# Mamba2's decays per head and RWKV's key preparation: work moved from GpSimd to VectorE in a two-layer decoder trunk

## The chip, the cores and the metric

The kernel runs on one core of a Trainium2 chip. A core has TensorE (PE in the rows: matmuls; PEld are its weight loads), VectorE (DVE), ScalarE (ACT), GpSimd (POOL) and SyncE (SP, which here issues the DMAs). Each works through its own queue in order and waits for others by semaphores. The metric is the device time of one execution, in microseconds (us), as the median over several runs.

## The reference

Two layers over x of 1024 positions and 1024 features, in float32. Each normalizes, projects to the inputs of three mixers, runs these, multiplies them by a SiLU gate, concatenates, projects back and adds. The first layer has RWKV-7, an S5 state-space model and attention to a memory of 256 entries; the second has Mamba-2, multi-head latent attention (MLA) and the memory attention. The change touches these parts of RWKV-7 and Mamba-2:

```python
def rwkv7_time_mix(p, mu, w0, w2, a0, a2, k_k, k_a, r_k, ln_w, ln_b):
    ...
    log_w = -jax.nn.softplus(-(w0 + jnp.tanh(w_lat) @ w2)) - 0.5
    decay = jnp.exp(-jnp.exp(log_w))
    iclr = jax.nn.sigmoid(a0 + a_lat @ a2)
    kk = (k * k_k).reshape(b, s, h, n).astype(jnp.float32)
    kk = (kk * lax.rsqrt(jnp.maximum(jnp.sum(kk * kk, -1, keepdims=True), 1e-24))).astype(p.dtype)
    k = k * (1.0 + (iclr - 1.0) * k_a)
    ...
    removal = kk * iclr
    def step(state, inp):
        r_t, w_t, k_t, v_t, kk_t, b_t = inp
        sa = -jnp.einsum('bhij,bhj->bhi', state, kk_t)
        state = (state * w_t[:, :, None, :] + sa[..., None] * b_t[:, :, None, :]
                 + v_t[..., None] * k_t[:, :, None, :])
        return state, jnp.einsum('bhij,bhj->bhi', state, r_t)
    ...

def mamba2_ssd(xbc, dt_raw, z, conv_w, conv_b, dt_bias, a_log, d_skip, norm_w):
    ...
    a_cum = jnp.cumsum(a_dt, axis=-1)
    lmat = jnp.exp(segsum(a_dt))
    cb = jnp.einsum('bclgn,bcsgn->bgcls', cc, bc)
    y_diag = jnp.einsum('bgcls,bgjcls,bcsgjp->bclgjp', cb, lmat, xdt)
    decay_states = jnp.exp(a_cum[..., -1:] - a_cum)
    states = jnp.einsum('bcsgn,bgjcs,bcsgjp->bcgjpn', bc, decay_states, xdt)
    ...
    y_off = jnp.einsum('bclgn,bcgjpn,bgjcl->bclgjp', cc, states, jnp.exp(a_cum))
    y = (y_diag + y_off).reshape(b, s, h, p) + xh * d_skip[:, None]
```

`lmat` holds, for each head and chunk of 128 positions, the exponential of the difference of two running sums of the log decay, for a target and an earlier source position.

## The kernel before

**Matmuls.** Every float32 operand of a large product is split into a high and a low part (L405 on ScalarE, L406 on VectorE), and a product takes three matmuls. The large projections are the dense stream: weights w come in by DMA on SP's queue (L331), are split, and are multiplied (L180). The mixers' own products and transposes (L180, L184) stand between.

**What sets the order.** A planner (class Flow) runs the mixers as generators and fixes TensorE's order: each `yield` says how much planned time must pass on TensorE, or which event or PSUM bank must be there, before the generator goes on, and the dense stream fills what is free. TensorE's instructions keep that order. The order in the other engines' queues is set by a scheduler that knows the dependencies and estimated durations; a queue, once built, runs in order.

**RWKV** (about 70 to 950 us of the span). 16 units: eight pairs of heads, each in two halves of 512 positions. For each unit:

- `rw_prep0` makes keys, decays and the removal vectors. kh (tile tg) is the scaled key; its squares are summed per head on TensorE; L588 multiplies the reciprocal of the sum by kh (d2, tile tb). L600 clears a column of ce, L602 forms running sums of the log decays, L607 centres them (cc), and L611 and L613 take exponentials. L614 and L615 pick the factors at chunk ends (fin). L619, L621 and L623 build kr and bm from these; L621 needs L588's result. L624 (ScalarE) and L625 build the mixed key. `half_products` then has TensorE form products of bm and kr into ga.
- `rw_inv0` inverts small triangular blocks: four DMAs of ga to memory (L699), one back into ai (L702), GpSimd's copy L706 of a start value into ti, then 31 pairs of a product (L711) and a subtraction (L713) on ti, the DMA of ti to memory (L715), and four DMAs back into xt (L718). ti and ai have one buffer each.
- `rw_inv1` transposes parts of xt (L728, VectorE) and continues on TensorE.
- `rw_prep1` makes km (L665), and L666 and L668 further operands.
- `rw_seq` runs over the chunks and keeps the state; its L808 (ScalarE) evicts rh, which TensorE reads next.

So GpSimd does the inverses and, between them, L588, L600, L614, L615, L625 and L665.

**Mamba2** (about 1640 to 2090 us). Two groups of eight heads, eight chunks of 128 positions each: 16 calls of `m2_x` and `m2_y`. `m2_x` loads into lm the running sums of the chunk for eight heads, broadcast over the partitions (L1931, three buffers); eb is the exponential of a part of it (L1936). L1937 (GpSimd) subtracts the source position's running sum, one column per head broadcast along the row; L1938 (VectorE) takes the minimum with 0; L1939 (ScalarE) the exponential; L1941 multiplies by the masked product of C and B, on VectorE in odd chunks and on GpSimd in even ones. Then come xdt (L1946), xdec (L1956), and the new state sta (L1962, L1963). `m2_y` has TensorE form the outputs, and VectorE combines them: m2y (L1981, L1982) and xs (L1987, four per chunk). The stream `x()` calls `m2_x` for one chunk after the other.

Of the kernel before, what the change touches and what calls it, by code (L numbers as in the profile page):

```python
# [10 lines left out]
F32 = mybir.dt.float32  # L11
# [3 lines left out]
A = mybir.AluOpType  # L15
# [4 lines left out]
P = 128  # L20
# [245 lines left out]
class K:  # L266
# [303 lines left out]
    def rw_prep0(self, st, p, lat, l2, k, wk):  # L570


        nc, F = self.nc, self.flow
        b3 = lambda ap: ap.rearrange("p (b t) -> p b t", b=4)
        l2h, l2l = l2
        kh = self.pp.tile([P, HT], F32, name="tg", bufs=1)
        nc.scalar.mul(kh, k, self.col("rw_k_k", p))
        sq = self.pp.tile([P, HT], F32, name="tb", bufs=1)
        nc.scalar.square(sq, kh)
        parts = self.pp_parts(sq)  # L580
        yield [BK, ("g", 1)]
        ps = self.bank("g")
        self.head_sums(ps, parts)
        d2 = self.pp.tile([P, HT], F32, name="tb", bufs=1)
        nc.vector.tensor_scalar(d2, ps, 1e-24, None, A.max)
        F.rel("g", 2.0)
        nc.vector.reciprocal(d2, d2)
        nc.gpsimd.tensor_tensor(d2, d2, kh, A.mult)  # L588
        yield ("g", 2)
        pw, pa = self.bank("g"), self.bank("g")  # L590
        for i, o in enumerate((pw, pa)):
            for j, w in enumerate((l2h, l2l)):
                F.matmul(o, lhsT=w[:, i, :], rhs=lat[:, i], start=(j == 0), stop=(j == 1))
        tw = self.pp.tile([P, HT], F32, name="ta", bufs=1)
        nc.scalar.activation(tw, pw, AF.Tanh, bias=self.hw0[:, p:p + 1], scale=0.5)
        F.rel("g", 2.0)
        F.rel("g", 5.0)
        nc.scalar.activation(tw, tw, AF.Identity, bias=1.0)
        ce = self.pp.tile([P, 4, P + 1], F32, name="ce", bufs=1)
        nc.gpsimd.memset(ce[:, :, 0:1], 0.0)  # L600
        for b in range(4):
            nc.vector.tensor_tensor_scan(ce[:, b, 1:P + 1], self.rst, tw[:, b * P:(b + 1) * P], 0.0,  # L602
                                         A.mult, A.add)
        ic = self.pp.tile([P, HT], F32, name="ta", bufs=1)
        nc.scalar.activation(ic, pa, AF.Tanh, bias=self.hw0[:, 8 + p:9 + p], scale=0.5)
        cc = self.pp.tile([P, 4, P + 1], F32, name="cc", bufs=1)
        nc.vector.tensor_tensor(cc, ce, ce[:, :, 64:65].broadcast_to([P, 4, P + 1]), A.subtract)  # L607
        fin = wk.tile([P, 12], F32, name="fin", bufs=4)
        nc.scalar.activation(fin[:, 0:4], ce[:, :, 64], AF.Exp, scale=-KDEC)
        e = ce  # L610
        nc.scalar.activation(e, cc, AF.Exp, scale=-KDEC)  # L611
        em = cc[:, :, 1:P + 1]
        nc.scalar.activation(em, em, AF.Exp, scale=KDEC)  # L613
        nc.gpsimd.tensor_copy(fin[:, 4:8], e[:, :, P])  # L614
        nc.gpsimd.tensor_tensor(fin[:, 8:11], fin[:, 4:7], fin[:, 1:4], A.mult)  # L615
        nc.scalar.activation(ic, ic, AF.Identity, scale=0.5, bias=self.p5)

        kr = wk.tile([P, 4, 2, P], F32, name="kr", bufs=3)
        nc.vector.tensor_tensor(kr[:, :, 0, :], b3(kh), e[:, :, 0:P], A.mult)  # L619

        nc.vector.tensor_tensor(kh, d2, ic, A.mult)  # L621
        bm = b3(kh)
        nc.vector.tensor_tensor(bm, bm, em, A.mult)  # L623
        nc.scalar.activation(ic, ic, AF.Identity, scale=self.col("rw_k_a", p), bias=self.oka[:, p:p + 1])  # L624
        nc.gpsimd.tensor_tensor(k, ic, k, A.mult)  # L625

        ga = wk.tile([P, 4, 2, P], F32, name="ga", bufs=2)
        yield [HA, ("g", 2)]
        self.half_products(bm, kr, 0, ga)
        st.update(fin=fin, kr=kr, ga=ga, e=e, em=em, bm=bm, k2=k)  # L630
# [28 lines left out]
    def rw_prep1(self, st, p, r, v, wk):  # L659

        nc, F = self.nc, self.flow
        b3 = lambda ap: ap.rearrange("p (b t) -> p b t", b=4)
        kr, e, em, bm, k2 = (st[n] for n in ("kr", "e", "em", "bm", "k2"))
        km = st["km"] = wk.tile([P, 4, P], F32, name="km", bufs=2)
        nc.gpsimd.tensor_tensor(km, b3(k2), em, A.mult)  # L665
        nc.vector.tensor_tensor(kr[:, :, 1, :], b3(r), e[:, :, 1:P + 1], A.mult)  # L666

        nc.vector.scalar_tensor_tensor(k2, r, self.col("rw_r_k", p), k2, A.mult, A.mult)  # L668
        parts = self.pp_parts(k2)
        tok = st["tok"] = wk.tile([P, 3, 4, P], F32, name="tok", bufs=2)  # L670

        for i, src in ((0, b3(v)), (1, bm), (2, km)):
            if i == 2:
                yield [BL, ("g", 1)]
                bp = self.bank("g")
                self.head_sums(bp, parts)
                bon = st["bon"] = wk.tile([P, HT], F32, name="bon", bufs=2)
                nc.vector.tensor_tensor(bon, bp, v, A.mult)
                F.rel("g", 2.0)
            yield ("g", 1)  # L680
            tp = self.bank("g", (P, 4, P))
            for b in range(4):
                F.transpose(tp[:, b, :], src[:, b, :], self.ident)
            nc.scalar.copy(tok[:, i], tp)
            F.rel("g", 2.0)
        gr = st["gr"] = wk.tile([P, 4, 2, P], F32, name="gr", bufs=2)
        yield ("g", 2)
        self.half_products(bm, kr, 1, gr)
# [1150 lines left out]

    def m2_open(self, wk):  # L1840
        nc = self.nc
        self.m2w, self.nxs, self.cv, self.lacc = wk, 6, {}, {}
        self.hconv = wk.tile([P, 60], F32, name="hconv")
        o = COFF["conv0"]
        nc.vector.tensor_scalar(self.hconv, self.cols[:, o:o + 60], 0.5, None, A.mult)
        self.hm2n = wk.tile([P, 8], F32, name="hm2n")
        o = COFF["m2_norm_w"]
        nc.vector.tensor_scalar(self.hm2n, self.cols[:, o:o + 8], 0.5, None, A.mult)
        self.one = wk.tile([P, P], F32, name="one")
        nc.vector.memset(self.one, 1.0)  # L1850
        self.ones = {}
        for n in (2048, 384, 256):
            self.ones[n] = wk.tile([P, P], F32, name="ones%d" % n)
            nc.vector.memset(self.ones[n], 1.0 / n)
        self.mincl = wk.tile([P, P], F32, name="mincl")
        nc.gpsimd.memset(self.mincl, 1.0)
        nc.gpsimd.affine_select(out=self.mincl, in_=self.mincl, compare_op=A.is_ge, fill=0.0,
                                base=0, pattern=[[1, P]], channel_multiplier=-1)
        self.sel = wk.tile([P, P], F32, name="sel")
        nc.gpsimd.memset(self.sel, 0.0)  # L1860

        nc.gpsimd.affine_select(out=self.sel, in_=self.sel, compare_op=A.not_equal, fill=1.0, base=-127,
                                pattern=[[0, P]], channel_multiplier=1)
        self.tk = {n: wk.tile([P, 8, 16], F32, name="tk" + n) for n in ("ac", "dt", "et", "dd")}
# [36 lines left out]
    def m2_bc(self, g):  # L1901
# [5 lines left out]
        for c4 in range(0, 8, 4):  # L1907
# [11 lines left out]
            F.rel("g", 1.5)  # L1919
            F.rel("g", 2.0)  # L1920

    def m2_x(self, g, c, st):

        nc, F, wk, tk = self.nc, self.flow, self.m2w, self.tk
        tt, ptt = nc.vector.tensor_tensor, nc.gpsimd.tensor_tensor
        hs = slice(8 * g, 8 * g + 8)
        bc = lambda ap, n: ap[:, c, hs].unsqueeze(2).broadcast_to([P, 8, n])
        v3 = lambda ap: ap.rearrange("p (h q) -> p h q", h=8)
        s = slice(c * P, (c + 1) * P)
        lm = wk.tile([P, 8, P], F32, name="lm", bufs=3)  # L1930
        nc.sync.dma_start(lm, self.acd[hs, s].unsqueeze(0).broadcast_to([P, 8, P]))  # L1931
        eb = wk.tile([P, 4, P], F32, name="eb", bufs=2)
        l2 = lm.rearrange("p (r two) t -> p r two t", two=2)
        for i in range(2):
            r = slice(64 * i, 64 * i + 64)
            nc.scalar.activation(eb[r], l2[r, :, i], AF.Exp)  # L1936
        ptt(lm, lm, bc(tk["ac"], P), A.subtract)  # L1937
        nc.vector.tensor_scalar(lm, lm, 0.0, None, A.min)  # L1938
        nc.scalar.activation(lm, lm, AF.Exp)  # L1939
        cb = self.cbm[:, c].unsqueeze(1).broadcast_to([P, 8, P])  # L1940
        (tt if c % 2 else ptt)(lm, lm, cb, A.mult)  # L1941
        tp = self.bank("g")
        for i in range(4):
            F.transpose(tp[:, i * P:(i + 1) * P], self.cv[4 * g + i][:, s], self.ident)
# [10 lines left out]
        xd = wk.tile([P, 512], F32, name="xdec", bufs=2)  # L1955
        tt(v3(xd), v3(tp), bc(tk["dd"], 64), A.mult)  # L1956
        F.rel("g", 2.5)
        yield [3.0, ("g", 1)]
        sp = self.bank("g")
        F.matmul(sp, lhsT=self.btok[:, c], rhs=xd, start=True, stop=True)  # L1960
        nx = st["next"] = wk.tile([P, 512], F32, name="sta", bufs=3)
# [97 lines left out]
    def m2_streams(self):  # L2059
# [9 lines left out]
        def x():  # L2069
            for g in range(2):  # L2070
                yield [("conv", 8 + g), ("conv", 10 + g), "m2dt"]
                yield from self.m2_bc(g)
                F.done(("bc", g), 0)
                for c in range(8):
                    n = 8 * g + c
                    yield [("conv", 4 * g + 3), ("g", 1)] + ([("y", n - 2)] if n > 1 else [])
                    yield from self.m2_x(g, c, sts[g])
                    F.done(("x", n), 7.0)
# [402 lines left out]
```

## Time and profile before

| what | value |
|---|---|
| time of three runs | 2715.13, 2717.84 (median), 2728.02 us |
| the profiled execution's own time | 2720.39 us |
| its span, first to last instruction | 2718.5 us |
| mean granted TensorE clock | 0.956 of full |
| busy: PE | 2517.2 us (93%), 15058 instructions |
| busy: PEld | 2032.4 us (75%) |
| busy: DVE | 1747.5 us (64%), 3423 instructions |
| busy: ACT | 1248.3 us (46%) |
| busy: POOL | 670.2 us (25%), 1407 instructions |

A row of the profile names the source line (L588), the engine, the operation, and output <- inputs by the program's names, with the output's shape and type and the input's. "x16" is a count. In square brackets, or after a last bar, stands how long the engine had been idle before and what it waited for. "SPq" is a DMA queue of SP. The granted clock (PEclk) is a share of full speed.

### The profile page before, as it was taken

The numbers are of one execution on the slowest core, as the hardware profiler recorded it, in microseconds if no ns is written. First come the engines' busy times: TensorE is split into PE (matmuls) and PEld (weight loads), VectorE is DVE, ScalarE is ACT, GpSimd is POOL, SyncE is SP. The second block draws the span as 40 slices with busy tenths as digits, with TensorE's granted clock in tenths as the row PEclk, the third lists the DMA queues.
The fourth block names the chain that finished last, engine by engine and source line by source line (L and its number), as shares of the span: only waits on it lengthen the run. The fifth ranks groups of instructions, "written<-read, shape, count | busy, mean of one in ns | idle before, by whom it ended". The sixth has DMA issues, their size and how long they took to land. (4 is left out here: it accounts for less than half of the span.)

```text
span 2718.5 us, 42261 instructions
## 1 busy us (share of the span) xinstructions
PE 2517.2 (93%) x15058; PEld 2032.4 (75%) x15058; DVE 1747.5 (64%) x3423; ACT 1248.3 (46%) x2443; POOL 670.2 (25%) x1407
## 2 busy tenths in 40 slices
PE   7899999998999989988999998988999979998997
PEld 5777777786777877776778776767677768887786
DVE  9756666675665536776556357777733987777532
ACT  7444344443443333554443346435344646655443
POOL 3544543544345300010000111251311030000011
PEclk9989999999999989888999999999999999999999
DMA  4433233233332334464674564242445431114543
GB/s 152 130 93 96 90 96 104 86 90 89 95 104 59 88 119 143 137 211 131 196 235 138 165 189 123 71 124 73 109 149 180 142 112 57 57 50 134 179 136 99
DMA packets 263859, 328.27 MB, mean 121 GB/s; under 512 B 88016, under 2 KB 135248, under 8 KB 263136
## 3 DMA queue, kind: packets, MB, share of 16 engines
q1 hardware_dynamic: 260736, 319.39, 38.1%
q0 software_dynamic: 1280, 4.20, 0.5%
q8 instruction: 119, 1.95, 0.3%
q10 hardware_dynamic: 1632, 1.98, 0.3%
q14 instruction: 92, 0.75, 0.1%
HBM read 232.59 MB, written 92.90 MB: 120 GB/s over the span
## 5 line engine op out<-in xcount | busy, mean ns | idle before, releaser
L406 DVE TENSOR_TENSOR wl<-w,wh 128x512 fp32r<-128x512 f32 (+2 forms) x410 | 279.6, 685 | 294.2 <-ACT wh L405 285.8
L405 ACT CAST wh<-w 128x512 fp32r<-128x512 f32 (+2 forms) x410 | 242.2, 594 | 389.1 <-PE mm L180 251.1
L180 PE MATMUL mm<-xhi,wh 128*128 128x512 f32 x832 | 363.0, 436 | 13.2 <-ACT xhi L474 6.8
L180 PE MATMUL mm<-xlo,wh 128*128 128x512 f32 x832 | 339.3, 408 | 4.8 <-DVE xlo L497 2.4
L180 PE MATMUL mm<-xhi,wl 128*128 128x512 f32 x832 | 337.4, 406 | 0.0
L180 PE MATMUL mm<-x1h,wh 128*128 128x512 f32 (+1 forms) x608 | 252.5, 415 | 24.6 <-ACT craw L1829 14.8
L180 PE MATMUL mm<-x1h,wl 128*128 128x512 f32 (+1 forms) x608 | 241.8, 398 | 0.0
L180 PE MATMUL mm<-x1l,wh 128*128 128x512 f32 (+1 forms) x608 | 241.5, 397 | 0.0
L711 POOL TENSOR_TENSOR titmp<-ai,ti 128x60 f32<-128x60 f32 (+24 forms) x496 | 159.9, 322 | 299.8 <-DMA ai<-d_in 262.5
L180 PEld LDWEIGHTS mm<-xhi,wh 128*128 128x128 f32 x832 | 162.2, 195 | 66.8 <-issue 19.9
L180 PEld LDWEIGHTS mm<-xhi,wl 128*128 128x128 f32 x832 | 162.3, 195 | 39.4
L180 PEld LDWEIGHTS mm<-xlo,wh 128*128 128x128 f32 x832 | 162.9, 196 | 36.6 <-DVE xlo L475 5.5
L713 POOL TENSOR_TENSOR ti<-ti,titmp 128x60 f32<-128x60 f32 (+24 forms) x496 | 163.8, 330 | 38.6
L180 PEld LDWEIGHTS mm<-x1h,wh 128*128 128x128 f32 (+1 forms) x608 | 116.8, 192 | 57.1 <-ACT craw L1829 17.6
L180 PEld LDWEIGHTS mm<-x1l,wh 128*128 128x128 f32 (+1 forms) x608 | 116.7, 192 | 27.5 <-issue 3.9
L180 PEld LDWEIGHTS mm<-x1h,wl 128*128 128x128 f32 (+1 forms) x608 | 116.3, 191 | 26.7 <-DVE wl L406 0.2
L180 PE MATMUL mm<-yb,wh 128*128 128x512 f32 x320 | 103.7, 405 | 5.2 <-ACT yb L405 3.8
L800 ACT ACTIVATE sn<-s0c,fin 64x64 f32<-64x64 f32 x128 | 44.1, 345 | 105.5 <-DVE s0c L828 58.3
L786 DVE TENSOR_TENSOR gb<-g,m 128x256 f32<-128x256 f32 x128 | 49.4, 417 | 58.3 <-PE g L180 58.0
L1680 POOL TENSOR_TENSOR sq<-sq,sqt 128x512 f32<-128x512 f32 x14 | 18.1, 1291 | 246.3 <-DMA w<-in_w_ev_out 161.1
L180 PEld LDWEIGHTS mm<-yb,wh 128*128 128x128 f32 x320 | 61.4, 192 | 21.7 <-ACT yb L405 4.2
L419 DVE SCALAR_TENSOR_TENSOR ev<-ev,mm 128x512 f32<-128x512 f32 x72 | 49.0, 681 | 42.7 <-ACT ev L418 42.3
(598 smaller groups left out, 6329.1 us busy)
## 6 DMA issues: line engine op xcount, KB each, us to landing
w<-in_w_ev_in SPq DMA_DIRECT2D x106, 256.0 KB
w<-in_w_od_in SPq DMA_DIRECT2D x82, 256.0 KB
w<-in_w_ev_out SPq DMA_DIRECT2D x64, 256.0 KB
w<-in_w_od_out SPq DMA_DIRECT2D x64, 256.0 KB
rd<-ev SPq DMA_DIRECT2D x50, 256.0 KB
spl<-yd SPq DMA_DIRECT2D x40, 256.0 KB
zod<-ev SPq DMA_DIRECT2D x36, 256.0 KB
ai<-d_in SPq DMA_DIRECT2D x16, 512.0 KB
```

Source lines behind the costliest of these rows:

```text
L180: return self._pe(self.nc.tensor.matmul(out, lhsT=lhsT, rhs=rhs, start=start, stop=stop, **kw), math.prod(rhs.shape[1:]), rhs.dtype)
L405: self.nc.scalar.copy(hi, src)
L406: self.nc.vector.tensor_tensor(lo, src, hi.bitcast(F32), A.subtract)
L419: nc.vector.scalar_tensor_tensor(g, g, 1.0, ps, A.add, A.mult)
L711: eng.tensor_tensor(tm, ai[:, s:s + 1, s + 1:32].broadcast_to([P, n, w]), ti[:, 0:n, s:s + 1].broadcast_to([P, n, w]), A.mult)
L713: eng.tensor_tensor(ti[:, 0:n, s + 1:32], ti[:, 0:n, s + 1:32], tm, A.subtract)
L786: nc.vector.tensor_tensor(gb[:, h], pgs[h], self.m2, A.mult)
L800: nc.scalar.mul(sg[hs], sc[hs, hs], g[hs])
L1680: nc.gpsimd.tensor_tensor(self.sq1, self.sq1, t, A.add)
```

## The change

In RWKV six instructions go from GpSimd to VectorE: L588, L600, L614, L615, L625 and L665. What they compute is unchanged. In Mamba2 the subtraction and the minimum become eight VectorE instructions per chunk, one per head, with the head's column as a per-partition scalar and both operations in one; the mask product is on VectorE in every chunk. The load of lm is asked for one chunk ahead by a new function. Three planned times change: 5.0 in place of 3.0 before the state product, and new waits of 6.0 at the start of the second group and 8.0 before the first chunk of the first. Lines behind L1921 have numbers 6 or 7 higher in the changed kernel (L1987 becomes L1994).

```diff
@@ rw_prep0
-        nc.gpsimd.tensor_tensor(d2, d2, kh, A.mult)
+        nc.vector.tensor_tensor(d2, d2, kh, A.mult)
...
-        nc.gpsimd.memset(ce[:, :, 0:1], 0.0)
+        nc.vector.memset(ce[:, :, 0:1], 0.0)
...
-        nc.gpsimd.tensor_copy(fin[:, 4:8], e[:, :, P])
-        nc.gpsimd.tensor_tensor(fin[:, 8:11], fin[:, 4:7], fin[:, 1:4], A.mult)
+        nc.vector.tensor_copy(fin[:, 4:8], e[:, :, P])
+        nc.vector.tensor_tensor(fin[:, 8:11], fin[:, 4:7], fin[:, 1:4], A.mult)
...
-        nc.gpsimd.tensor_tensor(k, ic, k, A.mult)
+        nc.vector.tensor_tensor(k, ic, k, A.mult)
@@ rw_prep1
-        nc.gpsimd.tensor_tensor(km, b3(k2), em, A.mult)
+        nc.vector.tensor_tensor(km, b3(k2), em, A.mult)
@@ m2_open
-        self.m2w, self.nxs, self.cv, self.lacc = wk, 6, {}, {}
+        self.m2w, self.nxs, self.cv, self.lacc, self.lms = wk, 6, {}, {}, {}
@@ new function
+    def m2_lm(self, g, c):
+        lm = self.lms[g, c] = self.m2w.tile([P, 8, P], F32, name="lm", bufs=3)
+        src = self.acd[8 * g:8 * g + 8, c * P:(c + 1) * P]
+        self.nc.sync.dma_start(lm, src.unsqueeze(0).broadcast_to([P, 8, P]))
@@ m2_x
-        lm = wk.tile([P, 8, P], F32, name="lm", bufs=3)
-        nc.sync.dma_start(lm, self.acd[hs, s].unsqueeze(0).broadcast_to([P, 8, P]))
+        lm = self.lms.pop((g, c))
+        if (g, c) != (1, 7):
+            self.m2_lm(*divmod(8 * g + c + 1, 8))
...
-        ptt(lm, lm, bc(tk["ac"], P), A.subtract)
-        nc.vector.tensor_scalar(lm, lm, 0.0, None, A.min)
+        for h in range(8):
+            nc.vector.tensor_scalar(lm[:, h], lm[:, h], tk["ac"][:, c, 8 * g + h:8 * g + h + 1], 0.0, A.subtract, A.min)
         nc.scalar.activation(lm, lm, AF.Exp)
         cb = self.cbm[:, c].unsqueeze(1).broadcast_to([P, 8, P])
-        (tt if c % 2 else ptt)(lm, lm, cb, A.mult)
+        tt(lm, lm, cb, A.mult)
...
-        yield [3.0, ("g", 1)]
+        yield [5.0, ("g", 1)]
@@ x()
             for g in range(2):
                 yield [("conv", 8 + g), ("conv", 10 + g), "m2dt"]
+                if g == 0:
+                    self.m2_lm(0, 0)
+                yield 6.0 * g
                 yield from self.m2_bc(g)
                 F.done(("bc", g), 0)
+                yield 8.0 * (1 - g)
```

GpSimd's queue in RWKV, between the end of one unit's inverse and the start of the next, before:

```order
L711 TENSOR_TENSOR titmp<-ai,ti 128x8
L713 TENSOR_TENSOR ti<-ti,titmp 128x8
L706 COPY ti<-t_558 128x256
L588 TENSOR_TENSOR tb<-tb,tg 128x512
L614 COPY fin<-ce 128x4
L615 TENSOR_TENSOR fin<-fin 128x3
L625 TENSOR_TENSOR rk<-ta,rk 128x512
L665 TENSOR_TENSOR km<-rk,cc 128x512
L711 TENSOR_TENSOR titmp<-ai,ti 128x31
L713 TENSOR_TENSOR ti<-ti,titmp 128x31
```

The same place in the changed kernel:

```order
L711 TENSOR_TENSOR titmp<-ai,ti 128x8
L713 TENSOR_TENSOR ti<-ti,titmp 128x8
L706 COPY ti<-t_558 128x256
L711 TENSOR_TENSOR titmp<-ai,ti 128x31
L713 TENSOR_TENSOR ti<-ti,titmp 128x31
```

Nothing is left between the copy that opens an inverse and its first step. VectorE's queue in one RWKV unit, as a piece of the difference:

```order
+L588 TENSOR_TENSOR tb<-tb,tg 128x512
 L607 TENSOR_TENSOR cc<-ce 128x516
 L828 SCALAR_TENSOR_TENSOR s0c_584<-g,fin,sn_7122 64x64 x2
+L614 COPY fin<-ce 128x4
 L619 TENSOR_TENSOR kr<-tg,ce 128x4x128
 L666 TENSOR_TENSOR kr<-rr,ce 128x4x128
+L615 TENSOR_TENSOR fin<-fin 128x3
 L621 TENSOR_TENSOR tg<-tb,ta 128x512
 L563 TENSOR_SCALAR bd<-mm,cols 128x1
 L566 SCALAR_TENSOR_TENSOR ev<-mm,cols,ev 128x511
 L623 TENSOR_TENSOR tg<-tg,cc 128x512
+L625 TENSOR_TENSOR rk<-ta,rk 128x512
```

L588 now stands ahead of L607, on the engine that also runs L621, which reads its result. The other rows keep their order. VectorE's queue around a chunk of Mamba2, before:

```order
L1938 TENSOR_SCALAR lm<-lm 128x1024
L1981 TENSOR_TENSOR m2y<-g,eb 128x512
L1982 TENSOR_TENSOR m2y<-m2y,g 128x512
L1963 TENSOR_TENSOR sta<-sta,g 128x512
L1987 SCALAR_TENSOR_TENSOR xs<-xs,cols,m2y 128x128 x4
L1946 TENSOR_TENSOR xdt<-g,tkdt 128x512
L1956 TENSOR_TENSOR xdec<-g,tkdd 128x512
L406 TENSOR_TENSOR wl<-w,wh 128x512
L419 SCALAR_TENSOR_TENSOR ev<-ev,mm 128x512
L1963 TENSOR_TENSOR sta<-sta,g 128x512
L1938 TENSOR_SCALAR lm<-lm 128x1024
L1941 TENSOR_TENSOR lm<-lm,cbm 128x1024
```

In the changed kernel, where L1945 is the instruction per head, L1948 the mask product, and L1988, L1989 and L1994 are L1981, L1982 and L1987 of before:

```order
L1945 TENSOR_SCALAR lm<-lm,tkac 128x128 x3
L1994 SCALAR_TENSOR_TENSOR xs<-xs,cols,m2y 128x128 x4
L1945 TENSOR_SCALAR lm<-lm,tkac 128x128 x5
L406 TENSOR_TENSOR wl<-w,wh 128x512
L419 SCALAR_TENSOR_TENSOR ev<-ev,mm 128x512
L1988 TENSOR_TENSOR m2y<-g,eb 128x512
L1948 TENSOR_TENSOR lm<-lm,cbm 128x1024
L1989 TENSOR_TENSOR m2y<-m2y,g 128x512
L1945 TENSOR_SCALAR lm<-lm,tkac 128x128 x2
L1970 TENSOR_TENSOR sta<-sta,g 128x512
L1945 TENSOR_SCALAR lm<-lm,tkac 128x128 x6
```

The eight instructions of a chunk stand among those of another chunk's output, and the mask product stands between the two halves of m2y.

## Rows read from the trace of the kernel before

**Rows 1.** Waits of VectorE, 60 to 950 us: total us, times, longest.

```profile
DVE tg L621 <- POOL tb L588: 37.5, 9, 6.6
DVE cc L607 <- POOL ce L600: 25.7, 13, 5.6
```

**Rows 2.** Timeline, 674 to 680 us: start us, duration us, instruction, idle before, releaser.

```profile
675.29 0.40 POOL L706 COPY ti<-t 128x256 f32<-128x256 f32 x1 [4.89 <-DMA d_out<-ti]
675.65 1.26 POOL L588 TENSOR_TENSOR tb<-tb,tg 128x512 f32<-128x512 f32 x1
676.94 0.69 DVE L621 TENSOR_TENSOR tg<-tb,ta 128x512 f32<-128x512 f32 x1 [6.62 <-POOL tb L588]
...
678.70 1.11 PE L180 MATMUL g<-rh,xt 128*128 128x64 f32 x4 [5.97 <-ACT rh L808]
```

**Rows 3.** Five stretches: us, busy PE, PEld, DVE, ACT, POOL, PEclk, DMA, GB/s.

```profile
124.00:157.00 33.00, 23.79 (x169) 18.16 (x168) 12.15 (x22) 10.61 (x21) 12.96 (x31) 0.74 0.33 90
297.00:308.00 11.00, 6.75 (x67) 5.29 (x69) 4.26 (x9) 2.69 (x7) 3.45 (x5) 0.69 0.61 179
455.00:485.00 30.00, 24.75 (x194) 19.27 (x192) 14.68 (x38) 9.11 (x20) 9.36 (x24) 0.66 0.33 94
619.00:683.00 64.00, 53.14 (x404) 42.08 (x403) 39.59 (x85) 23.90 (x51) 31.08 (x75) 0.92 0.35 100
780.00:847.00 67.00, 58.60 (x440) 46.41 (x440) 39.21 (x84) 25.49 (x56) 29.71 (x75) 0.92 0.34 95
```

**Rows 4.** RWKV units, products to L728: three quiet, then nine stalled, with sums.

```profile
517.30:568.40 51.10, 51.10 (x426) 41.25 (x425) 37.12 (x82) 21.25 (x46) 23.97 (x68) 1.00 0.29 89
...
sum 155.90, PE 155.49 PEld 125.62 DVE 108.18 ACT 66.31 POOL 72.82; mean PE 51.83 PEld 41.88 DVE 36.06 ACT 22.10 POOL 24.27
...
626.50:685.10 58.60, 52.39 (x412) 41.79 (x411) 38.71 (x83) 23.30 (x50) 26.45 (x70) 0.93 0.33 96
...
sum 516.00, PE 473.36 PEld 376.80 DVE 316.08 ACT 209.13 POOL 236.79; mean PE 52.60 PEld 41.87 DVE 35.12 ACT 23.24 POOL 26.31
```

**Rows 5.** Timeline of SP's DMA queue: the inverse's way back in two units.

```profile
561.97 2.64 SPq L718 DMA_DIRECT2D xt<-d_out  x4
...
675.19 1.80 SPq L718 DMA_DIRECT2D xt<-d_out  x4
```

**Rows 6.** Tile ti: minimum, median, maximum ns, first and last start.

```profile
L711 POOL TENSOR_TENSOR titmp<-ai,ti x496: 209/291/866, 108.7 to 940.1; 128x60 f32<-128x60 f32 x16, 128x28 f32<-128x28 f32 x12, 128x66 f32<-128x66 f32 x11, 128x48 f32<-128x48 f32 x10
```

**Rows 7.** Groups of VectorE by form: busy us, mean ns, idle before, releaser.

```profile
L621 DVE TENSOR_TENSOR tg<-tb,ta 128x512 f32<-128x512 f32 x16 | 11.0, 689 | 37.5 <-POOL tb L588 37.5
L2232 DVE TENSOR_SCALAR pe<-pe,lsm 128x1024 f32<-128x1024 f32 x8 | 6.1, 767 | 0.2
L2232 DVE TENSOR_SCALAR pe<-pe,lsm 128x256 f32<-128x256 f32 x8 | 2.8, 345 | 0.0
L1938 DVE TENSOR_SCALAR lm<-lm 128x1024 f32<-128x1024 f32 x16 | 16.0, 1000 | 12.3 <-POOL lm L1937 12.3
L1941 DVE TENSOR_TENSOR lm<-lm,cbm 128x1024 f32<-128x1024 f32 x8 | 12.8, 1601 | 2.9 <-ACT lm L1939 2.9
L1987 DVE SCALAR_TENSOR_TENSOR xs<-xs,cols,m2y 128x128 f32<-128x128 f32 x64 | 37.7, 646 | 0.1
```

**Rows 8.** Groups of GpSimd by form, in Mamba2.

```profile
L1937 POOL TENSOR_TENSOR lm<-lm,tkac 128x1024 f32<-128x1024 f32 x16 | 31.4, 1965 | 24.0 <-ACT eb L1936 21.5 <-ACT tkac L1889 2.5
L1941 POOL TENSOR_TENSOR lm<-lm,cbm 128x1024 f32<-128x1024 f32 x8 | 20.6, 2578 | 17.8 <-ACT lm L1939 12.0 <-DVE cbm L1917 5.8
```

**Rows 9.** Line L1987's instructions: minimum, median, maximum ns.

```profile
L1987 DVE SCALAR_TENSOR_TENSOR xs<-xs,cols,m2y x64: 332/340/2466, 1761.2 to 1990.6; 128x128 f32<-128x128 f32 x64
```

**Rows 10.** Two stretches of Mamba2, columns as in the five stretches.

```profile
1740.00:1835.00 95.00, 84.95 (x473) 66.51 (x472) 72.75 (x105) 34.82 (x53) 45.56 (x31) 0.95 0.43 117
1905.00:1985.00 80.00, 70.79 (x421) 55.13 (x420) 58.72 (x84) 33.61 (x48) 30.57 (x19) 0.98 0.42 116
```

**Rows 11.** Waits of ScalarE, 1640 to 2090 us.

```profile
ACT eb L1936 <- DMA lm<-acd: 33.9, 8, 8.4
```

## The prediction

> **What bounds the kernel now.** I read the busy times first, then the chain of waits, the stretches where TensorE idles, the waits by engine, and the timeline around each gap. TensorE runs an order fixed at build time and is busy for 93% of the span, so only its idle time and the time at the lower granted clock can be won; the reader is to see which engine ends its waits.
>
> In the RWKV part the waits lead to GpSimd. VectorE waits 37.5 us in 9 places for the product of L588, the longest 6.6 us, and 25.7 us in 13 places at L607 for the little memset of L600 [rows 1]. One such place, instruction by instruction [rows 2]: GpSimd's queue is in order, and its copy L706, which opens the next inverse, waits 4.89 us for the transfer that carries the last inverse out. L588, ready long before, stands behind that copy and takes 1.26 us. VectorE (L621) has waited 6.62 us for it; ScalarE's L624 needs what VectorE makes, L808 stands behind L624 in ScalarE's queue, and TensorE, which needs L808's rh, stood still for 5.97 us. Five stretches hold nearly all such places [rows 3]. They last 33 + 11 + 30 + 64 + 67 = 205 us and TensorE is busy for 167.0 of them: 38.0 idle. Their granted clock is 0.74, 0.69, 0.66, 0.92 and 0.92, where a stretch without a gap shows 1.00 [rows 4]. A lost tenth of a stretch is a tenth of its time, so this is 8.6 + 3.4 + 10.2 + 5.1 + 5.4 = 32.7 us at the 1.2 GHz level. Together 70.7 us, of which 1.86 us for each us of idleness.
>
> In Mamba2 GpSimd's subtraction L1937 (1965 ns) and its mask product L1941 (2578 ns) [rows 8] slow VectorE, which works beside them: L1987 has a median of 340 ns but reaches 2466 [rows 9], and its mean is 646 [rows 7]. Two stretches hold most of TensorE's losses there [rows 10]: 95 + 80 us with 84.95 + 70.79 busy, so 19.3 idle, and 95 x 0.05 + 80 x 0.02 = 6.4 of clock: 25.7 us.
>
> **RWKV: six instructions to VectorE.** TensorE's order is unchanged there. After the change GpSimd holds nothing but inverses, so nothing waits behind L706 any more: the 70.7 us are the gross gain. What is late next is the inverse itself: products to memory, GpSimd's 62 instructions, result back, transposes at L728. Three units without a large stall show what a unit takes with that chain in it: 51.10 us with TensorE always busy and the clock at 1.00 in one, 155.90 over the three, 51.97 each [rows 4]. Nine stalled units take 516.00, 57.33 each. If they become like the three, 516.0 - 9 x 51.97 = 48.3 us go. That is 22.4 less than 70.7; part of the difference lies in the unit ahead of the nine. So the chain takes back between 0 and 22.4 us; I take 18, near the upper end, because the units' rows measure it.
>
> On VectorE each of the 16 units gets L588, L625 and L665, at the 689 ns that L621 takes with the same shape [rows 7], and three tiny ones. A per-column operation takes 345 ns for 256 elements and 767 for 1024 [rows 7], so 0.55 ns an element and some 204 ns before the first. Per unit 3 x 0.69 + 3 x 0.2 = 2.7 us, in all 43. Bounds on TensorE's path: 0, since VectorE is busy for 37.12 us of the quiet unit's 51.10 and TensorE doesn't wait there [rows 4], to all 43. I take 8, a fifth, nearer to that row: L588 stands at the head of the chain to the next products, the others have slack. A gain from VectorE no longer being slowed beside GpSimd's big products lies within the choice. RWKV: 70.7 - 18 - 8 = 45 us.
>
> A rule of the Trainium skill (SBUF — State Buffer, "Who interferes with whom") speaks against this: a VectorE instruction with two SBUF inputs and a GpSimd one that reads SBUF lock each other out, and the later one waits for the whole of the other. By it the three moved products, 2.1 us a unit, could each hold up an inverse step; over 16 units 33 us on the inverse chain, and the sum would be 2693. The spread of L711, 291 ns in the median and 866 at most [rows 6], agrees that it happens.
>
> **Mamba2: decays per head on VectorE.** Removed from GpSimd: 16 subtractions and 8 mask products. VectorE gets 128 instructions of 128 elements: 204 + 128 x 0.55 = 274 ns each, an estimate from the two rows of L2232, so 35.1 us; 8 mask products at 1601 ns, 12.8 us; it loses 16 minima of 1000 ns [rows 7]. It also has a new wait: in the even chunks too the mask product now stands in VectorE's queue behind ScalarE's exponential, and m2y's second half and L1987's successors behind it. For the same wait VectorE shows 2.9 us in 8 chunks [rows 7], GpSimd 12.0 [rows 8]: I take 5. Relief: L1987's 64 instructions cost 37.7 us where 64 medians are 21.8, so up to 16 us; half, 8, since the other half may come from other neighbours. Net 35 + 13 - 16 + 5 - 8 = 29 us more VectorE, over 16 chunks, where it idles 22.3 + 21.3 us in the two stretches [rows 10].
>
> What TensorE gains from it: at best all 25.7 us; at worst nothing, and the 29 us land on it. I take half of the gain, 13: the gaps that VectorE's slowed instructions cause should go, those that wait for the load of lm stay. ScalarE waits 33.9 us for that load in 8 places [rows 11]. It is now asked for a chunk earlier in the program, but it has the same three buffers, each freed by TensorE, and in SP's queue it stands where it stood, with weight loads behind it: I take nothing. The ends are a gain within the 25.7 us, and a loss of one such wait, 8.4 us [rows 11], if a weight load comes to stand behind a load of lm. The waits of 6 and 8 units at the start of each group only set where TensorE's planner puts the first chunk: in TensorE's order its transposes come after 81 matmuls of the dense stream in both kernels. Between pairs of chunks, 45 dense matmuls now stand where 36 stood, unevenly, so the chunks are spread over a longer time: cover for the 29 us.
>
> **Sum.** 2720.4 (the profiled execution's own time, 1.9 above its span) - 45 - 13 = 2662. The median of the runs, 2717.84, is 2.6 below the profiled one, so 2660.
>
> **Rivals.**
> 1. The inverse is late in every unit. For it: from its products to the first result transfer unit 10 takes 675.19 - 626.50 = 48.7 us, the quiet unit 561.97 - 517.30 = 44.7 [rows 4, 5], so units may come out at 51.97 + 4.0 = 56.0. Then 9 x (57.33 - 55.97) = 12 us go, less 8, and with Mamba2's 13 the time is 2701. Against it: in three units it did not happen. The skill's rule above would end between this and the forecast.
> 2. VectorE becomes the bound, and the kernel slower. Added are 43 us in RWKV and 35 + 13 - 16 + 5 = 37 in Mamba2, 80 in all. If each landed on TensorE with its clock, 80 x 1.86 = 149 us would stand against 70.7 + 25.7 = 96: 53 more, 2771. It decides from 96 / 1.86 = 52 us, two thirds of the added work. Against it: VectorE idles 14 us in a quiet unit [rows 4].
> 3. Mamba2 loses: VectorE is busy for 72.75 of 95 us [rows 10] and its 29 us land on TensorE. 2720.4 - 45 + 29 - 2.6 = 2702.
> 4. All losses go and nothing takes their place: 2720.4 - 96 - 2.6 = 2621.
> 5. The change moves queues but not the waits, if what L808 waits for is ScalarE's own order rather than L588: about 2717. Against it: in the row of L621 all 37.5 us end with L588 [rows 7].
>
> **How the numbers follow.** The forecast 0.62, with its own range 2635 to 2690; the late inverse 0.13 (2690 to 2706, most of it the skill's rule and the chain together); Mamba2 losing 0.06; all losses going 0.08; no change 0.04; VectorE the bound 0.07. The range to hold the time 8 times in 10 is 2618 to 2708: it takes in the 2621 and the two cases near 2702. A measurement of this kernel tells 0.5% from no change, 13.6 us, so faster is below 2704.2. Faster: 0.62 + 0.08 + 0.09 + 0.03 = 0.82. Same: 0.04 of the late inverse, 0.03 of Mamba2 losing, 0.04 without change: 0.11. Slower 0.07.
>
> **What would show it.** The waits of VectorE for GpSimd at L621, L607 and L668 are gone, and the five stretches' granted clock is near 1.00. TensorE's gaps that remain in RWKV end at the transposes of L728, up to 3 us each, and those up to 1.8 without a fall of the clock. L588 and its neighbours take about 0.7 us on VectorE, and L711 keeps its median near 291 ns; at over 330 the lock-out of the two engines is real. In Mamba2 the per-head instructions take near 0.27 us and L1994 (L1987 before) keeps to its median. It would be wrong if VectorE is busy for over 45 us of a unit, or if TensorE waits for VectorE's lm in Mamba2 more than it does now.

## The result and the profile after

The changed kernel takes 2695.24 us (median of 4 runs, 2688.09 to 2699.3), the kernel before 2722.93 (4 runs, 2715.13 to 2743.78). The ratio is 0.9892, with a 95% interval of 0.9851 to 0.9933: 29 us faster (18 to 41). 58 us were forecast. The direction was right. The time lies inside the range of 2618 to 2708, but outside the forecast's own 2635 to 2690 and inside that of the first rival, the late inverse (2690 to 2706). Half of the gain is missing, and it is missing in RWKV.

Busy times of the changed kernel, from its page:

```profile
span 2697.5 us, 42287 instructions
...
PE 2520.6 (93%) x15058; PEld 2036.5 (75%) x15058; DVE 1771.6 (66%) x3639; ACT 1249.7 (46%) x2445; POOL 563.2 (21%) x1287
```

The work did move: GpSimd is busy for 107 us less, VectorE for 24 more. The waits that the change was to end are gone. Before, VectorE waited for GpSimd at L621 and L607 [rows 1], and at L668:

```profile
DVE rk L668 <- POOL km L665: 13.1, 6, 5.1
```

The changed kernel has none of the three, and L588 takes 700 ns on VectorE, as forecast. Groups of VectorE by form in the changed kernel:

```profile
L588 DVE TENSOR_TENSOR tb<-tb,tg 128x512 f32<-128x512 f32 x16 | 11.2, 700 | 0.0
...
L621 DVE TENSOR_TENSOR tg<-tb,ta 128x512 f32<-128x512 f32 x16 | 10.9, 680 | 0.0
...
L1945 DVE TENSOR_SCALAR lm<-lm,tkac 128x128 f32<-128x128 f32 x128 | 32.1, 315 | 6.4 <-ACT eb L1943 6.4
L1948 DVE TENSOR_TENSOR lm<-lm,cbm 128x1024 f32<-128x1024 f32 x16 | 20.3, 1271 | 1.8 <-ACT lm L1946 1.5
L1994 DVE SCALAR_TENSOR_TENSOR xs<-xs,cols,m2y 128x128 f32<-128x128 f32 x64 | 20.2, 374 | 0.0
```

L621's 37.5 us of waiting [rows 7] are 0.0 now. Yet TensorE got little of it. Two windows between the same instructions of TensorE in both kernels, the bulk of RWKV (6000 matmuls) and Mamba2 with what stands beside it (2300); columns as in [rows 3]. The kernel before:

```profile
143.50:948.70 805.20, 763.89 (x6001) 610.55 (x6000) 509.85 (x1101) 326.40 (x699) 374.35 (x1029) 0.96 0.31 91
1649.60:2167.80 518.20, 472.42 (x2302) 380.10 (x2301) 350.71 (x549) 247.86 (x410) 134.00 (x111) 0.96 0.39 120
```

The changed kernel:

```profile
135.40:954.60 819.20, 780.09 (x6002) 624.21 (x6001) 530.32 (x1182) 326.85 (x698) 322.19 (x946) 0.94 0.31 90
1645.50:2145.70 500.20, 468.71 (x2302) 378.07 (x2301) 347.35 (x669) 246.41 (x411) 87.00 (x87) 0.97 0.41 124
```

Mamba2 is 18 us shorter. RWKV starts 8 us earlier and ends 6 later: TensorE idles for 39.1 us there, 41.3 before, at a clock of 0.94 in place of 0.96. Single profiles scatter: the same RWKV code ended at 948.7 us here and at 962.5 in the profile of the kernel with Mamba2's part alone. So what RWKV is worth is taken from timed runs below. What the traces do show is that the wait moved. Waits of TensorE in that stretch (total us, times, longest), the kernel before:

```profile
PE g L180 <- ACT rh L808: 16.7, 4, 6.0
PE g L180 <- DVE xn L728: 12.4, 15, 2.5
PE g L180 <- DVE s0c L828: 9.6, 3, 4.7
```

and the changed kernel:

```profile
PE g L180 <- DVE xn L728: 35.4, 21, 7.2
PE g L180 <- ACT ta L616: 1.2, 1, 1.2
```

The waits for rh and s0c, at the end of the chain from L588, are gone, and the wait for L728, the transposes of the inverse's result, has grown from 12.4 to 35.4 us, with 7.2 for the longest. Here is that wait in unit 1, followed back through the queues (start us, duration us, instruction, idle before). First ScalarE's eviction of ga, from the timeline of the changed kernel:

```profile
130.95 1.07 ACT L654 COPY ga<-g 128x512 f32<-128x512 f32 x2
```

SP's queue:

```profile
135.43 0.57 SPq L715 DMA_DIRECT2D d_out<-ti  x1
...
140.16 1.80 SPq L718 DMA_DIRECT2D xt<-d_out  x4
...
144.50 2.08 SPq L699 DMA_DIRECT2D d_in<-ga  x4
...
149.33 0.54 SPq L702 DMA_DIRECT2D ai<-d_in  x1
...
186.04 0.56 SPq L715 DMA_DIRECT2D d_out<-ti  x1
...
190.77 1.81 SPq L718 DMA_DIRECT2D xt<-d_out  x4
```

GpSimd's inverse, then VectorE and TensorE behind it:

```profile
160.32 0.24 POOL L711 TENSOR_TENSOR titmp<-ai,ti 128x31 f32<-128x31 f32 x1 [19.66 <-DMA ai<-d_in]
```

```profile
192.50 1.40 DVE L728 STREAM_TRANSPOSE xn<-xt 32x256 f32<-32x256 f32 x3 [11.71 <-DMA xt<-d_out]
```

```profile
192.98 0.31 PE L180 MATMUL g<-xn,ga 32*32 32x32 f32 x2 [7.25 <-DVE xn L728]
```

ga is there at 132.0. The DMAs that carry it out (d_in) stand in SP's queue behind the last unit's d_out and xt, which wait for the last inverse, and the last of them is issued by 146.6; the load of ai takes 11.0 us from its issue to the first step, the inverse 25.7, the way back 6.5. TensorE waits for all of it. Averaged over the 16 units, worked out from the timelines of both kernels: from ga to the issue of the last d_in it takes 2.5 us before and 5.0 after, the inverse takes 25.1 and 26.0, and between the last issue of xt and TensorE's use of it 6.0 us were left and 2.9 are.

### The profile page after: what moved, and what is told of

It is laid out like the page before. It is cut to its first block, busy times and chain, and to the rows that moved or that the text cites. A ratio compares the mean times of both kernels' runs of the same rounds, so it can differ in the third digit from the quotient of the medians.

```text
span 2697.5 us, 42287 instructions
## 1 busy us (share of the span) xinstructions
PE 2520.6 (93%) x15058; PEld 2036.5 (75%) x15058; DVE 1771.6 (66%) x3639; ACT 1249.7 (46%) x2445; POOL 563.2 (21%) x1287
## 5 line engine op out<-in xcount | busy, mean ns | idle before, releaser
L406 DVE TENSOR_TENSOR wl<-w,wh 128x512 fp32r<-128x512 f32 (+2 forms) x410 | 273.9, 672 | 295.7 <-ACT wh L405 291.4
L711 POOL TENSOR_TENSOR titmp<-ai,ti 128x60 f32<-128x60 f32 (+24 forms) x496 | 167.4, 338 | 412.1 <-DMA ai<-d_in 374.5
L713 POOL TENSOR_TENSOR ti<-ti,titmp 128x60 f32<-128x60 f32 (+24 forms) x496 | 171.5, 346 | 38.8
L180 PEld LDWEIGHTS mm<-x1h,wh 128*128 128x128 f32 (+1 forms) x608 | 115.6, 190 | 55.3 <-ACT craw L1829 19.5
L800 ACT ACTIVATE sn<-s0c,fin 64x64 f32<-64x64 f32 x128 | 44.1, 345 | 98.7 <-DVE s0c L828 55.8
L180 PE MATMUL g<-xn,ga 32*32 32x32 f32 (+1 forms) x768 | 39.0, 225 | 37.4 <-DVE xn L728 35.4
```

The lines of the kernel that those rows point to most:

```text
L180: return self._pe(self.nc.tensor.matmul(out, lhsT=lhsT, rhs=rhs, start=start, stop=stop, **kw), math.prod(rhs.shape[1:]), rhs.dtype)
L406: self.nc.vector.tensor_tensor(lo, src, hi.bitcast(F32), A.subtract)
L711: eng.tensor_tensor(tm, ai[:, s:s + 1, s + 1:32].broadcast_to([P, n, w]), ti[:, 0:n, s:s + 1].broadcast_to([P, n, w]), A.mult)
L713: eng.tensor_tensor(ti[:, 0:n, s + 1:32], ti[:, 0:n, s + 1:32], tm, A.subtract)
L800: nc.scalar.mul(sg[hs], sc[hs, hs], g[hs])
```

## The experiments

All times are medians; each kernel's ratio is to the kernel before, run beside it on its chip. The changed kernel was timed beside a kernel before of 2722.93 us, the kernels compared with it below beside others, of 2721.73 to 2731.72. So its differences from them, 59, 55 and 65 us below, are surer by the ratios: 61, 52 and 62 us, each to within about 17.

### The two parts apart

RWKV alone, on the kernel before: the six instructions of the change, of which two stand here, nothing else.

```diff
-        nc.gpsimd.tensor_tensor(d2, d2, kh, A.mult)
+        nc.vector.tensor_tensor(d2, d2, kh, A.mult)
...
-        nc.gpsimd.tensor_tensor(km, b3(k2), em, A.mult)
+        nc.vector.tensor_tensor(km, b3(k2), em, A.mult)
```

> Only the six RWKV instructions are moved to VectorE; Mamba2 is as before. Theory A, formed on the two traces (the inverse's way from ga to xt ends nearly every unit once GpSimd's queue is free, and was already a hair's breadth behind the stalls): the RWKV part gains nothing, ratio 0.998 to 1.004 (in the trace of the changed kernel the last RWKV unit ends 6 us later than before). Rival B, the forecast's account: 45 us faster, ratio 0.983, with Mamba2's part giving little in the whole change.

Measured 2711.72 us, ratio 0.9945 (0.9919 to 0.9971): 15 us faster (8 to 22). Between the two theories: more than nothing, a third of the forecast's 45. In its trace TensorE waits for L728 for 38.9 us in RWKV and no longer for rh, as in the changed kernel.

Mamba2 alone: the changed kernel with those six back on GpSimd.

```diff
-        nc.vector.tensor_tensor(d2, d2, kh, A.mult)
+        nc.gpsimd.tensor_tensor(d2, d2, kh, A.mult)
...
```

> Only the Mamba2 part of the change; RWKV is as before. Theory A: Mamba2 gives the whole gain, 19 to 27 us, ratio 0.990 to 0.993 (between the same two places of TensorE's order the changed kernel takes 19 us less there). Rival B: 13 us, ratio 0.995.

Measured 2704.89, ratio 0.9911 (0.9881 to 0.9941): 24 us (16 to 32), where the forecast had 13. The sum of the two, 39, agrees with the whole change's 18 to 41.

### A shorter inverse, after and before

Each inverse stops after 22 of its 31 steps; the last nine are left out.

```diff
-        for s in range(31):
+        for s in range(22):
```

In the changed kernel:

> The changed kernel with each inverse cut after 22 of its 31 steps, which takes 7.5 us (by the trace) from each of the 16 inverses; the rest of the inverse is left out. Theory A (the inverse's way ends the units): 3 to 7 us go from each unit, 50 to 110 us faster than the changed kernel, and TensorE's gaps ahead of the transposes' matmuls are gone. Rival C (VectorE's added work is what TensorE waits for): within 10 us of the changed kernel.

Measured 2636.10, ratio 0.9667 (0.9619 to 0.9715): 59 us faster than the changed kernel, with VectorE's work unchanged. Waits of TensorE for L728 fell to

```profile
PE g L180 <- DVE xn L728: 7.6, 7, 3.2
```

from 35.4 us. So the inverse's way ended the units, and VectorE's added work did not. The same cut in the kernel before:

> The kernel before, with each inverse cut after 22 of its 31 steps (6.9 us less by its trace; the rest of the inverse is left out), as in the cut of the changed kernel, which gained 2.2% over it. Theory A (also before the change the inverse's loop set the pace, and GpSimd's stalls at L588 were one face of it): 50 to 90 us faster than before, ratio 0.967 to 0.982, nearly the cut of the changed kernel plus Mamba2's 24 us. Rival B (before, the stalls in GpSimd's queue set the pace by themselves): under 25 us, ratio over 0.991.

Measured 2673.60, ratio 0.9820 (0.9776 to 0.9865): 49 us faster. A cut that leaves the six instructions where they were, in GpSimd's queue behind the inverse, takes 49 of the 70.7 us that the queue seemed to cost. That is theory A, just at the lower end of its range. In its trace the wait at L621, 37.5 us before [rows 1], is nearly gone, though L588 was not moved:

```profile
DVE tg L621 <- POOL tb L588: 7.4, 2, 3.7
```

The cut also takes 7.2 us of work a unit out of GpSimd's own queue, so alone it does not tell whether the queue was too full or the inverse too late. The load in pieces, below, leaves that work as it is.

### SP's queue

```diff
-            nc.sync.dma_start(d_in[i].rearrange("(b h) s t -> s b h t", h=2), ga[q, :, :, q])
+            nc.scalar.dma_start(d_in[i].rearrange("(b h) s t -> s b h t", h=2), ga[q, :, :, q])
```

> The changed kernel, but the four DMAs that carry ga to memory (L699) are issued on ScalarE's queue, right behind the evictions that make ga, in place of SP's queue, where they stand behind the DMAs of the previous inverse's result. Theory A1 (the next inverse waits in SP's queue for the last one): the mean time from ga to the last of these DMAs falls from 5.0 to about 1.5 us a unit, and 2 to 3 us go in each of the 16 units, with clock: 30 to 60 us faster than the changed kernel, 2640 to 2665. Rival A2 (the inverse itself, lengthened by VectorE beside it, from 25.1 to 26.0 us, is what took the gain): 0 to 10 us. Rival C (VectorE's added work is the bound): no change, 2695.

Measured 2682.12, ratio 0.9855 (0.9778 to 0.9931), not to be told from the changed kernel's. The mean from ga to the last d_in is 4.8 us in its trace, 5.0 in the changed kernel: the edit did not take away the wait that it was meant to take away. Unit 1 in its trace:

```profile
139.15 1.80 SPq L718 DMA_DIRECT2D xt<-d_out  x4
141.38 2.95 ACTq L699 DMA_DIRECT2D d_in<-ga  x4
144.43 0.69 ACT L561 ACTIVATE ev<-mm,omu 128x512 f32<-128x512 f32 x1 [12.71 <-DMA d_in<-ga]
```

On ScalarE's queue d_in still comes behind the last unit's xt: by the trace's semaphores it waits there for one that a DMA of xt raises as it lands, at 141.31 us. ScalarE is held up with it, for 12.71 us. So the run tells nothing for or against A1, and how much SP's queue costs stays open.

### Only the two releases moved

The changed kernel with L614, L615, L625 and L665 back on GpSimd.

```diff
-        nc.vector.tensor_tensor(k, ic, k, A.mult)
+        nc.gpsimd.tensor_tensor(k, ic, k, A.mult)
...
-        nc.vector.tensor_tensor(km, b3(k2), em, A.mult)
+        nc.gpsimd.tensor_tensor(km, b3(k2), em, A.mult)
```

> The changed kernel with only L588 and L600, for which VectorE had waited, on VectorE; L614, L615, L625 and L665 are back on GpSimd. Theory A1 (VectorE's products beside the inverse lengthen it by 0.9 us a unit, and that costs): the mean inverse falls from 26.0 to about 25.4 us, 5 to 15 us faster than the changed kernel, unless L625 and L665, again between the inverses, hold up ga or L668: then 0 to 15 us slower, with waits for km at L668 of some 13 us in the trace. Rival C (it is VectorE's load): 10 to 25 us faster.

Measured 2687.03, ratio 0.9881 (0.9833 to 0.9928): the same as the changed kernel. The mean inverse is 25.5 us as expected, and VectorE waits 32.3 us for km at L668, where some 13 were expected. The time is the same, but the waits of TensorE are others (100 to 950 us):

```profile
PE g L180 <- ACT rh L808: 17.6, 4, 6.9
PE mm L180 <- DVE ev L419: 11.9, 1, 11.9
PE g L180 <- DVE xn L728: 11.8, 15, 3.7
```

The waits for L728 fell from 35.4 us to 11.8, and those for rh are back, with L588 on VectorE. The longest of them goes back through ScalarE's queue to L668, and from there to km, which stands behind L706 on GpSimd; the one for ev goes back to fin (L615), for which ScalarE waits 17.2 us. So the wait left L728 and came back at GpSimd's queue, and the time stayed.

### The load of ai in pieces

```diff
-        nc.sync.dma_start(ai.rearrange("p s t -> p (s t)"), bass.AP(d.tensor, d.offset, [[0, 4], *d.ap]))
+        for lo, hi in ((0, 4), (4, 10), (10, 18), (18, 32)):
+            d = d_in.rearrange("i b s t -> (i b) (s t)")[:, 32 * lo:32 * hi]
+            nc.sync.dma_start(ai[:, lo:hi].rearrange("p s t -> p (s t)"), bass.AP(d.tensor, d.offset, [[0, 4], *d.ap]))
```

This takes about as much from the inverse's way as the cut, but leaves nothing out. With two pieces, (0, 8) and (8, 32):

> The changed kernel with the load of ai in two DMAs, of the first 8 and the other 24 rows, so that the first inverse steps start when the first has landed. Nothing is left out. Theory A (the inverse's way ends the units): the time from the issue of ai to the first step falls from 10.2 us to 5 to 7, 3 to 5 us go from each of 16 units, 30 to 60 us faster than the changed kernel, 2635 to 2665. Rival C (VectorE's added work is the bound): within 10 us of it.

With four:

> As the load in two, but in four DMAs (4, 6, 8 and 14 rows). Theory A: the first step starts 4 to 6 us after the issue; 5 to 25 us faster than the load in two if the later pieces land in time, the same if the steps then wait for them or the extra DMAs in SP's queue hold up others. Rival C: as the changed kernel.

Measured 2639.65 us with two pieces, ratio 0.9701 (0.9657 to 0.9745), and 2629.98 with four, 0.9664 (0.9615 to 0.9713): 55 and 65 us faster than the changed kernel. The kernel with four pieces once more:

> The changed kernel with the load of ai in four DMAs once more, on the same chip as the other three: 2620 to 2640, ratio 0.962 to 0.972. It is the partner of the kernel with the six instructions back on GpSimd.

Measured 2628.03, ratio 0.9653 (0.9607 to 0.9699). In that trace the same unit's load and first step, on SP and GpSimd (the loop over the pieces shifts the lines behind it by two, L711 to L713):

```profile
141.03 2.21 SPq L704 DMA_DIRECT2D ai<-d_in  x4
```

```profile
143.99 0.43 POOL L713 TENSOR_TENSOR titmp<-ai,ti 128x31 f32<-128x31 f32 x1 [11.36 <-DMA ai<-d_in]
```

The first step starts 3.0 us after the issue, 11.0 in the changed kernel; averaged over the 16 units 3.1 and 10.2. RWKV's window between the same instructions of TensorE, and the waits for L728 (now L730):

```profile
135.90:889.90 754.00, 747.95 (x6001) 599.35 (x6000) 524.40 (x1172) 325.67 (x696) 304.65 (x944) 0.98 0.34 99
```

```profile
PE g L180 <- DVE xn L730: 3.6, 5, 1.2
```

754 us in place of 819, 6.1 idle in place of 39.1, and the clock at 0.98. Against the 805.2 of the kernel before, that is the whole gain that the forecast gave to the six instructions, with VectorE nearly as busy as in the changed kernel (524 and 530 us).

### What the six instructions are worth then

The kernel with four pieces and Mamba2's part, but the six RWKV instructions back on GpSimd:

```diff
-        nc.vector.tensor_tensor(d2, d2, kh, A.mult)
+        nc.gpsimd.tensor_tensor(d2, d2, kh, A.mult)
...
```

> The load of ai in four, with the Mamba2 part of the change, but the six RWKV instructions back on GpSimd. Against the same kernel with them on VectorE, run beside it, this shows what the RWKV part is worth when the inverse no longer ends the units. Theory A (the forecast's gross gain was there, but the inverse stood right behind it): 30 to 60 us slower than with them on VectorE, 2660 to 2690, with VectorE waiting for GpSimd's L588 again. Rival D (the stalls in GpSimd's queue were only a face of the inverse's loop and go with the earlier inverse by themselves): within 15 us of it, 2625 to 2645.

Measured 2637.43, ratio 0.9682 (0.9633 to 0.9730), against 2628.03 with them on VectorE: 9 us, and the intervals overlap, so this is not clear of noise. This is rival D. Against Mamba2's part alone (ratio 0.9911), the load in pieces gives 62 us by the ratios, with the six instructions on GpSimd in both. Waits of VectorE for GpSimd in RWKV, and the window:

```profile
DVE rk L668 <- POOL km L665: 10.1, 5, 5.0
DVE tg L621 <- POOL tb L588: 6.0, 3, 2.9
```

```profile
135.70:901.50 765.80, 754.05 (x6002) 604.61 (x6001) 513.35 (x1095) 324.78 (x697) 373.23 (x1029) 0.98 0.33 97
```

The wait for L588 is 6.0 us where it was 37.5 [rows 1], that for L600 is gone, and nothing in GpSimd's queue was moved. L588 was late because the inverse ahead of it ended late.

### The parts of Mamba2

Decays per head and the mask product alone, on the kernel before, with its loads and planned waits:

```diff
-        ptt(lm, lm, bc(tk["ac"], P), A.subtract)
-        nc.vector.tensor_scalar(lm, lm, 0.0, None, A.min)
+        for h in range(8):
+            nc.vector.tensor_scalar(lm[:, h], lm[:, h], tk["ac"][:, c, 8 * g + h:8 * g + h + 1], 0.0, A.subtract, A.min)
...
-        (tt if c % 2 else ptt)(lm, lm, cb, A.mult)
+        tt(lm, lm, cb, A.mult)
```

> The kernel before with only the decays per head and the mask product on VectorE; the load of lm and the planned waits stay as before. Theory A (GpSimd's two big products were what slowed VectorE, and that is Mamba2's gain): ratio 0.989 to 0.994, near the whole Mamba2 part's 0.991. Rival E (the chunks had to be spread out as well): under 8 us, ratio 0.997 to 1.003, with TensorE waiting for lm's mask product.

Measured 2707.69, ratio 0.9933 (0.9908 to 0.9957): 18 us (12 to 25). The early load of lm and the planned waits alone, also on the kernel before:

```diff
-        lm = wk.tile([P, 8, P], F32, name="lm", bufs=3)
+        lm = self.lms.pop((g, c))
+        if (g, c) != (1, 7):
+            self.m2_lm(*divmod(8 * g + c + 1, 8))
...
-        yield [3.0, ("g", 1)]
+        yield [5.0, ("g", 1)]
...
+                yield 6.0 * g
...
+                yield 8.0 * (1 - g)
```

> The kernel before with only the load of lm a chunk ahead and the three planned waits; the decays stay on GpSimd and VectorE. Theory A: nothing, ratio 0.997 to 1.003. Rival E (the spread of the chunks hides the waits): ratio 0.990 to 0.996.

Measured 2710.77, ratio 0.9955 (0.9925 to 0.9985): 12 us (4 to 20). Mamba2's window between the same instructions, with the decays alone and then with the waits alone:

```profile
1660.80:2160.10 499.30, 465.85 (x2301) 376.31 (x2300) 349.07 (x676) 249.60 (x414) 87.29 (x87) 0.98 0.40 125
```

```profile
1635.20:2137.50 502.30, 467.47 (x2301) 376.24 (x2300) 347.81 (x557) 247.97 (x414) 134.84 (x111) 0.97 0.41 124
```

Before it was 518.2, with both it is 500.2. In these windows, single profiles, either alone does nearly all of it. TensorE's waits for xdec (L1956), 10.6 us before, are 2.7 with the decays alone and 5.2 with the waits alone. The decays alone take away what slows VectorE: xs took 646 ns in the mean [rows 7] and takes 433, where the waits alone leave it at 595. The waits alone put 24 dense matmuls, in place of 15, between most chunks' transposes and the state product; that this covers VectorE's delay is argued, not shown, and the early load was not taken apart from the waits. The decays alone land where theory A had them, the waits alone where rival E had them, so each does something by itself. Whether 18 and 12 add up to the 24 of both (16 to 32) these times do not tell.

## Why the prediction was half right

**What bounds it.** Wrong at the root. The rows were right, TensorE stood still for rh behind L588 [rows 2], but the 70.7 us were put down to GpSimd's queue because it ended the waits. What delays that queue is its own inverse. From ga through SP, the load of ai, GpSimd and back, one inverse follows the last, and L706 and L588 stand behind it. Three kernels show it: the cut before (49 us), the cut after (59) and the load in pieces (65) win what the forecast gave to the move, and the move on top of the last is worth 9, not clear of noise.

**The step that failed** is "the chain takes back between 0 and 22.4 us; I take 18". RWKV alone is worth 15 us, so of 70.7 gross, less the 8 for VectorE, the chain took back about 48. The gross was itself counted high: the 32.7 us of clock are a loss, not time at the 1.2 GHz level, and were taken over whole stretches, waits included. Over the 167.0 us in which TensorE was busy they come to 25.6, an estimate from the same rows [rows 3]; the gross is then 63.6, and about 41 were taken back. The quiet units [rows 4] were read as units that run with the chain in them, which is right, but also as what the stalled ones would become. In the changed kernel a unit takes 55.8 us from its products to TensorE's use of the inverse, averaged over 16, and 55.3 before: where the products come earlier, d_in waits longer behind the last unit's transfers (5.0 us in place of 2.5), and TensorE then waits at L728. A wait that is removed gives back only what lies between it and the next one, and here only 6.0 us a unit lay there, part of it needed. The sentence that the remaining gaps end at L728 was right, their size, up to 3 us, was not: the two longest are 6.5 and 7.2. Nor did the clock come near 1.00: it is 0.94 in RWKV's window.

**VectorE's 8 of 43.** Not contradicted, and not measured by itself: VectorE is busy for 20 us more in RWKV's window, where 43 were counted, and with the load in pieces the same queue runs 754 us with 6.1 idle.

**The lock-out of VectorE and GpSimd** (the Trainium skill, SBUF — State Buffer, "Who interferes with whom") was priced at up to 2.1 us a unit. The mean inverse went from 25.1 to 26.0, at most 14 us over 16 units, and L711's median from 291 to 296 ns, well under the 330 named. With the load in pieces the inverse is 24.8 us with the six instructions on VectorE and 24.7 with them on GpSimd. The rule may hold for single instructions; it did not decide the time. That its 2693 lies next to the measured 2695 is luck: it has 33 us on the inverse.

**Mamba2's 13** were mis-sized: 24 (16 to 32). The instruction per head takes 315 ns, not 274, but L1948 takes 1271, not 1601, and L1994 is down to 374 ns from 646, 17.5 us in all, where 8 was counted. VectorE's busy time in the window fell, 350.7 to 347.4, where 24 more were expected (29 with 5 of waiting). And the early load with the planned waits, put at nothing, is worth 12 us alone. This error hides a part of the other: 11 us too little here, 30 too much in RWKV. That the sum stayed inside the range owes something to it.

**The rivals.** Rival 1, the late inverse, was right in its mechanism, and its 56.0 us a unit are close to the 55.8 measured; it got 0.13. Its time of 2701 comes from 4 us for RWKV and 13 for Mamba2, where the parts alone gave 15 and 24. It was argued away with three units in which it "did not happen"; why their result came back 4 us sooner than that of unit 10 no run shows. Rival 2, VectorE the bound, is refuted by the cuts, which leave VectorE's work as it was.

## What to carry to other kernels

When a wait ends with an engine's queue, ask what delays the head of that queue before counting the wait as the queue's cost: if it is a loop (here inverse, SP, load, inverse), moving the instructions behind it can mostly move the wait to the loop's other exit (here 15 us of a forecast 45 were left). A test that costs little is to shorten the suspected loop in the kernel before, with nothing moved. And a chain's length is not read from units in which the wait did not show; it is followed through every queue, from its input to its use.

## What was not expected of the hardware

A 512 KB load that a chain waits for can be cut where its reader works through it in order: averaged over 16 units, the first step came 3.1 us after the issue with four DMAs and 10.2 us with one, and the inverse was not slowed (24.8 us, 26.0 with one DMA).

The forecast let gaps of up to 1.8 us pass without a fall of the clock, as a wait of TensorE of 1.80 us at 349.70 did in the kernel before. In the changed kernel these waits,

```profile
636.83 0.22 PE L180 MATMUL g<-xn,ga 32*32 32x32 f32 x2 [1.42 <-DVE xn L728]
637.72 0.47 PE L180 MATMUL g<-xn,ga 32*32 32x32 f32 x17 [0.67 <-DVE xn L728]
```

were followed by the 1.2 GHz level (granted clock 0.50, columns as in [rows 3]; the first row is ahead of them):

```profile
625.00:635.00 10.00, 10.00 (x69) 8.04 (x69) 7.99 (x17) 4.81 (x10) 4.54 (x10) 1.00 0.09 13
639.60:653.30 13.70, 13.70 (x111) 10.62 (x110) 7.35 (x22) 3.24 (x7) 0.00 (x0) 0.50 0.60 156
```

Two waits, 2.1 us together, and 13.7 us at half speed behind them. RWKV's window in the changed kernel has four such places, with no single wait over 1.5 us, and they hold 48 of the 106 us that it spends at the 1.2 GHz level; the kernel before spends 61 there. So RWKV's clock could fall from 0.96 to 0.94 while its idle time did not grow.
